# The first norm's modulation by blocks of 128 features, and with each block its rows of the convolution's projections in float32

## The chip, the cores and the metric

The kernel runs on one core of a Trainium2 chip. The metric is the device time of one execution in microseconds (us), the median of three runs. The engines are named as in the profile: PE is TensorE (matmuls; PEld is its weight load), DVE is VectorE, ACT is ScalarE, POOL is GpSimd, and SP is SyncE, which issues the loads.

## The reference

A token matrix x of 256 tokens by 1024 features passes through two layers and then through a second, wider block. Every norm of the two layers is modulated by columns that come from a vector c. Cut to the part that matters here:

```python
c_act = jax.nn.silu(c)
for layer in range(2):
    mod = (c_act @ ada_w[layer] + ada_b[layer])[:, None, :]
    shift_m, scale_m, gate_m, shift_f, scale_f, gate_f = jnp.split(mod, 6, axis=-1)
    h = _rmsnorm(x, norm_g[layer, 0]) * (1.0 + scale_m) + shift_m
    ...                      # layer 0: gated convolution and retention on h @ w_in; layer 1: S5
    x = x + gate_m * mix
    h = _rmsnorm(x, norm_g[layer, 1]) * (1.0 + scale_f) + shift_f
    x = x + gate_f * (jnp.square(jax.nn.relu(h @ w_fc1[layer])) @ w_fc2[layer])
```

`ada_w` has 1024 x 6144 numbers for each layer, so a layer's modulation is 24 MB of float32 weights for six vectors of 1024. In layer 0 `h @ w_in` has 3072 columns; the first 1024 are the convolution's values (512) and its gates (512), the rest are q, k, v and the gate of the retention. The convolution has 31 taps over 512 channels.

## The kernel before

All activations lie with features on the 128 partitions, in eight blocks of 128 features, 256 tokens along the row. A weight is loaded in pieces of 1 MB (`load`, into one of four buffers of the pool `wr`) by SyncE, and split into two float32r parts (`split`, `hilo`): ScalarE rounds a quarter to `hi` (L314), VectorE subtracts to get `lo` (L315), in two buffers each. A projection (`lin`, `mm3`, L319 to L321) is then three matmuls for every block of features and 128 columns, so 48 matmuls for a piece.

A vector of the modulation (`ada`, L434 to L447) is four loads of 1 MB, here called four steps. Each step is eight matmuls into 32 partitions of a PSUM bank (L439); behind the fourth VectorE transposes the sums (L444) and adds the bias (L445). The ten vectors that are not needed at once are a fill (`Fill`): `step_piece` in the mixer makes 1.25 steps of it with every weight piece, the layer norm makes five at its start (`fills[0]`), the feed-forward of layer 0 makes 0.375 with every piece, and a call of `need` makes all steps up to a vector that is about to be used. The vector (1,5) is made in another way, by VectorE, far later.

The program begins with S5's parameters (`s5_prep`, small operations on VectorE and ScalarE, until about 51 us), then the scale and the shift of layer 0 (eight steps), the first norm (`rms`, `normed`), and then `mixer0`: four pieces for the convolution, in PSUM banks of the tag `mm`, with a tanh and a product (L518, L519) behind each pair; the 31 taps of the convolution, two channel blocks on ScalarE and GpSimd (L536, L537) and two on VectorE (L531, L533); eight pieces for q, k, v and the gate; the layer norm over the convolution's channels (L611 are its sums, float32 matmuls of full size); and the output projection. The text numbers the twelve pieces 0 to 11; 4 is the first of q.

What order the engines follow is set by a list scheduler: the code's order is the priority, and an instruction whose inputs are late in the scheduler's own reckoning lets later ones pass. On the chip each engine then takes its list strictly in order, SyncE too.

## Time and profile before

| | us |
|---|---|
| median of the runs | 1231.36 |
| lowest and highest run | 1228.97, 1233.6 |
| span of the profiled execution, from its first to its last instruction | 1227.2 |
| TensorE busy in that span | 1169.7 |
| VectorE busy | 891.7 |
| ScalarE busy | 609.7 |

The profile gives the span of one execution; no time of that very execution is given beside the span. The median of the runs lies 4.2 us above it. A matmul's busy time in the profile overlaps with that of the next one, so TensorE's busy share says whether it had work, and its pace is read from the distance between starts.

### The profile page before, as it was taken

How to read it: one execution, taken by the hardware profiler on the slowest of the kernel's cores; microseconds unless marked ns; L12 is line 12 of the kernel's file. 1: busy time of each engine (PE TensorE's matmuls, PEld its weight loads, DVE VectorE, ACT ScalarE, POOL GpSimd, SP SyncE). 2: the span in 40 equal slices, each digit the busy share in tenths (PEclk: the TensorE clock that was granted, in tenths of full speed). 3: DMA queues.
4: the chain of work that ended last, by engine and by line, in shares of the span. 5: the costliest groups of instructions: out<-in, count | busy, mean ns of one | idle time of the engine just before them, and what ended most of it. 6: DMA issues, size and time to landing. Idle time of an engine off the chain costs nothing. (4 is left out here: it accounts for less than half of the span.)

```text
span 1227.2 us, 25417 instructions
## 1 busy us (share of the span) xinstructions
PE 1169.7 (95%) x10482; PEld 1109.3 (90%) x10482; DVE 891.7 (73%) x1821; ACT 609.7 (50%) x1202; POOL 106.1 (9%) x138
## 2 busy tenths in 40 slices
PE   6899897999999976899999999999999999999998
PEld 4698686999999964899999999999999999999998
DVE  7879888889888859767765656686667686665564
ACT  3577244655555542545544545573465545544441
POOL 0077321000000006200000000000000000000000
PEclk8899997999999977799999999999999999999999
DMA  9888886688888999554466655453443454555541
GB/s 341 340 311 327 297 294 212 238 265 282 297 287 267 300 249 309 216 172 171 169 243 212 233 174 172 164 172 104 151 159 138 172 168 148 194 179 177 194 155 60
DMA packets 69979, 267.29 MB, mean 218 GB/s; under 512 B 7380, under 2 KB 35428, under 8 KB 43240
## 3 DMA queue, kind: packets, MB, share of 16 engines
q1 hardware_dynamic: 69864, 265.68, 63.5%
q8 instruction: 82, 1.34, 0.4%
q14 instruction: 33, 0.27, 0.1%
HBM read 246.85 MB, written 18.81 MB: 216 GB/s over the span
## 5 line engine op out<-in xcount | busy, mean ns | idle before, releaser
L315 DVE TENSOR_TENSOR lo<-w,hi 128x512 fp32r<-128x512 f32 (+1 forms) x640 | 427.6, 712 | 147.7 <-ACT hi L314 147.1
L314 ACT ACTIVATE hi<-w 128x512 fp32r<-128x512 f32 (+1 forms) x640 | 358.4, 625 | 337.0 <-PE mm L320 118.8
L319 PE MATMUL mm<-h,hi 128*128 128x256 f32 x1328 | 379.7, 286 | 0.3 <-ACT h L398 0.3
L320 PE MATMUL mm<-h,hi 128*128 128x256 f32 x1328 | 377.7, 285 | 1.3 <-DVE h L399 1.1
L321 PE MATMUL mm<-h,lo 128*128 128x256 f32 x1328 | 378.6, 285 | 0.0
L319 PEld LDWEIGHTS mm<-h,hi 128*128 128x128 f32 x1328 | 254.7, 192 | 7.2 <-issue 3.4
L320 PEld LDWEIGHTS mm<-h,hi 128*128 128x128 f32 x1328 | 254.6, 192 | 2.8 <-DVE h L399 1.5
L321 PEld LDWEIGHTS mm<-h,lo 128*128 128x128 f32 x1328 | 254.5, 192 | 2.6 <-issue 1.6
L321 PE MATMUL at<-s,lo 128*128 128x256 f32 x720 | 204.4, 284 | 1.7 <-DVE lo L315 1.7
L319 PE MATMUL at<-s,hi 128*128 128x256 f32 x720 | 204.8, 284 | 0.0
L320 PE MATMUL at<-s,hi 128*128 128x256 f32 x720 | 204.1, 284 | 0.0
L321 PEld LDWEIGHTS at<-s,lo 128*128 128x128 f32 x720 | 137.9, 192 | 2.5 <-DVE lo L315 2.1
L319 PEld LDWEIGHTS at<-s,hi 128*128 128x128 f32 x720 | 138.0, 192 | 1.8 <-issue 1.4
L320 PEld LDWEIGHTS at<-s,hi 128*128 128x128 f32 x720 | 138.0, 192 | 0.6 <-issue 0.6
L439 PE MATMUL fa<-wa,crep 128*32 128x256 f32 x704 | 56.4, 428 | 7.0 <-DMA wa<-in_ada_dram 3.8
L537 POOL TENSOR_TENSOR s<-s,cv 128x256 f32<-128x256 f32 x60 | 49.9, 866 | 38.9 <-ACT cv L536 38.7
L439 PEld LDWEIGHTS fa<-wa,crep 128*32 128x32 f32 x704 | 23.0, 120 | 27.0 <-issue 6.4
L319 PE MATMUL fp<-h,hi 128*128 128x256 f32 x144 | 41.9, 291 | 0.7 <-ACT h L314 0.7
L320 PE MATMUL fp<-h,hi 128*128 128x256 f32 x144 | 41.8, 290 | 0.0
L321 PE MATMUL fp<-h,lo 128*128 128x256 f32 x144 | 41.6, 289 | 0.0
L929 ACT COPY Wt<-fp 128x512 f32<-128x512 f32 x32 | 18.6, 581 | 43.3 <-PE fp L928 39.9
L536 ACT ACTIVATE cv<-ap,s 128x256 f32<-128x256 f32 x60 | 29.5, 506 | 17.2 <-POOL s L537 16.4
(438 smaller groups left out, 1829.6 us busy)
## 6 DMA issues: line engine op xcount, KB each, us to landing
w<-in_fc_dram SPq DMA_DIRECT2D x64, 1024.0 KB, 5.1
wa<-in_ada_dram SPq DMA_DIRECT2D x44, 1024.0 KB, 6.5
w<-in_w_in_dram SPq DMA_DIRECT2D x38, 1024.0 KB, 4.9
w<-in_w_gate_dram SPq DMA_DIRECT2D x11, 1024.0 KB, 5.0
w<-in_w_up_dram SPq DMA_DIRECT2D x11, 1024.0 KB, 4.9
Vd<-V SPq DMA_DIRECT2D x16, 512.0 KB, 6.6
w<-in_w_out_dram SPq DMA_DIRECT2D x8, 1024.0 KB, 6.2
Wd<-Wt SPq DMA_DIRECT2D x16, 512.0 KB, 5.2
```

What stands on the lines that cost most here:

```text
L314: self.nc.scalar.activation(hi, h, AF.Copy)
L315: self.nc.vector.tensor_tensor(lo, h, hi.bitcast(F32), op=ALU.subtract)
L319: mm(ps, sh, mh, start=start, stop=False, skip_group_check=True)
L320: mm(ps, sh, ml, start=False, stop=False, skip_group_check=True)
L321: mm(ps, sl, mh, start=False, stop=stop, skip_group_check=True)
L439: nc.tensor.matmul(ps[32 * q:32 * q + 32], self.crep[:, 2 * k + k2], w[:, n:n + 256], start=k == 0 and k2 == 0, stop=k == 3 and k2 == 1, t ...
L536: nc.scalar.mul(t, src, w)
L537: nc.gpsimd.tensor_tensor(acc[:, ch], acc[:, ch], t, op=ALU.add)
L929: nc.scalar.copy(W[:, :, k], pt.rearrange("p (e x) -> p e x", e=4))
```

## The change

The two steps "modulation" and "norm and the convolution's projections" are woven into one loop over the eight feature blocks (`first`). For a block c it loads the block's columns of scale and shift (`ada_c`, 1 MB) and the block's 128 rows of the convolution's 1024 weight columns (`w_in_a`, 0.5 MB, in a whole buffer of `wr`). It makes 256 modulation sums (eight matmuls, L494), copies them out on ScalarE (L496), turns them into two columns by two one-column matmuls against a vector that picks one row in 32 (L498), adds bias and gain on VectorE (L499, L500), norms the block (L502, L503), and adds the block's product with its weight rows into four PSUM banks, eight float32 matmuls (L505), without a split of the weights. The rounded h for the retention is made from the same h. The sums over all eight blocks are the convolution's values and gates (`pa`), and `mixer0` begins with the tanh on them. The first step of S5's preparation now comes ahead of all this in the code and the rest behind it. Lines move by 4 up to `ada`, and by more further on.

```diff
+    a = f(v["ada_w"])[0].reshape(8, 128, 6, 8, 128)[:, :, 0:2]
+    d["ada_c"] = con(a.transpose(3, 1, 0, 2, 4).reshape(8, 128, 2048))
+    d["w_in_a"] = con(f(v["w_in"])[0][:, 0:1024].reshape(8, 128, 1024))
...
+    def first(self, x, r):
+        nc = self.nc
+        pick = self.keep([128, 1], "pick")
+        nc.gpsimd.memset(pick, 0.0)
+        for q in range(4):
+            nc.gpsimd.memset(pick[32 * q:32 * q + 1], 1.0)
+        g = self.keep([128, 8], self.name("modg"))
+        cols = self.ps("mm")
+        pa = [self.pair("at") for _ in range(4)]
+        h32 = self.wh.tile([128, 2048], F32R, name="h32", tag="hi").bitcast(F32).rearrange("p (c t) -> p c t", c=8)
+        hh, hl = self.sb([128, 8, T], F32R, "h"), self.sb([128, 8, T], F32R, "h")
+        ab = self.col("ada_b", 0, 16)
+        for c in range(8):
+            wa = self.load(self.I["ada_c"][c].rearrange("p (k n) -> p k n", k=8), 8, 256)
+            w = self.load(self.I["w_in_a"][c].rearrange("p (k n) -> p k n", k=1), 1, 1024)
+            ps = self.ps(("fa", "fp")[c % 2])[:, 0:256]
+            for k in range(8):
+                q = 32 * (k % 4)
+                nc.tensor.matmul(ps[q:q + 32], self.crep[:, k], wa[:, k], start=k < 4, stop=k >= 4, tile_position=(0, q))
+            t = self.sb([128, 256])
+            nc.scalar.copy(t, ps)
+            for i in range(2):
+                nc.tensor.matmul(cols[:, 2 * c + i:2 * c + i + 1], t[:, 128 * i:128 * i + 128], pick, start=True, stop=True)
+            nc.vector.tensor_tensor(self.mod[0][:, c:c + 9:8], cols[:, 2 * c:2 * c + 2], ab[:, c:c + 9:8], op=ALU.add)
+            nc.vector.scalar_tensor_tensor(g[:, c:c + 1], self.mod[0][:, 8 + c:9 + c], 1.0, self.col("norm_g", c), op0=ALU.add, op1=ALU.mult)
+            h = self.sb([128, T])
+            nc.vector.scalar_tensor_tensor(h, x[:, c], g[:, c:c + 1], r, op0=ALU.mult, op1=ALU.mult)
+            nc.scalar.activation(h32[:, c], h, AF.Identity, bias=self.mod[0][:, c:c + 1])
+            for b in range(8):
+                nc.tensor.matmul(pa[b // 2][:, b % 2], w[:, 0, 128 * b:128 * b + 128], h32[:, c], start=c == 0 and b % 2 == 0,
+                                 stop=c == 7 and b % 2 == 1, skip_group_check=True)
+            self.hilo(hh[:, c], hl[:, c], h32[:, c])
+        return (hh, hl), pa
...
-    def mixer0(self, x, h, fill, need, after_conv, each):
+    def mixer0(self, x, h, pa, fill, need, after_conv, each):
...
         for j in range(2):
-            pv, pg = self.pair(), self.pair()
-            self.lin(pv, step_piece("w_in", j), h, K8)
-            self.lin(pg, step_piece("w_in", 2 + j), h, K8)
+            pv, pg = pa[j], pa[2 + j]
             t = self.sb([128, 2, T])
             nc.scalar.activation(t, pg, AF.Tanh, scale=0.5)
...
+            prep.step()
+            self.mark("first")
+            self.pc_tag = self.pb_tag = "mm"
+            h, pa = self.first(x, self.rms(x))
+            self.pc_tag = self.pb_tag = "at"
             self.mark("prep")
             prep.drain()
...
-            Fill(self.ada(0, 1), self.ada(0, 0)).drain()
...
-                h = self.normed(x, self.rms(x), self.modg(0, 1, 0), self.modv(0, 0))
...
-                self.mixer0(x, h, ada, lambda: need(0, 2), begin, lambda j: st.add(x))
+                self.mixer0(x, h, pa, ada, lambda: need(0, 2), begin, lambda j: st.add(x))
```

The four pieces that leave `mixer0` took five steps of the fill with them, so the fill's later calls find more left. What the scheduler makes of it on the engines is read from the built programs. Names carry a number for each tile; xN is a row repeated N times.

**TensorE at the start.** Before, behind the norm's sums (L167) come four steps of the scale, the spread of the norm's factor (L369), four of the shift and the first step of the fill:

```order
L439 MATMUL fa_367<-wa_368,crep 32x256 x8
L167 MATMUL at_468<-inv_99,q_479 128x1 x4
L439 MATMUL fa_367<-wa_378,crep 32x256 x8
L439 MATMUL fa_367<-wa_388,crep 32x256 x8
L439 MATMUL fa_367<-wa_398,crep 32x256 x8
L369 MATMUL at_503<-ident,s_491 128x128 x2
L439 MATMUL fa_411<-wa_412,crep 32x256 x8
L439 MATMUL fa_411<-wa_422,crep 32x256 x8
L439 MATMUL fa_411<-wa_432,crep 32x256 x8
L439 MATMUL fa_411<-wa_442,crep 32x256 x8
```

Now (behind the same sums, of which the first three groups and two modulations stand ahead of these rows) `fa` and `fp` hold a block's modulation sums, `mm_213` the columns, `at_214` to `at_217` the four banks; `w_285` and `w_317` are the modulation weights of blocks 2 and 3, `w_223` and `w_255` the weight rows of blocks 0 and 1:

```order
L494 MATMUL fa_289<-w_285,crep 32x256 x8
L373 MATMUL mm_203<-ident,s_191 128x128 x2
L498 MATMUL mm_213<-pick,s_234 128x1 x2
L498 MATMUL mm_213<-pick,s_266 128x1 x2
L494 MATMUL fp_321<-w_317,crep 32x256 x8
L505 MATMUL at_214<-h_218,w_223 128x256 x2
L505 MATMUL at_215<-h_218,w_223 128x256 x2
L505 MATMUL at_216<-h_218,w_223 128x256 x2
L505 MATMUL at_217<-h_218,w_223 128x256 x2
L498 MATMUL mm_213<-pick,s_298 128x1 x2
L505 MATMUL at_214<-h_218,w_255 128x256 x2
L505 MATMUL at_215<-h_218,w_255 128x256 x2
```

The matmuls of block 0 (`w_223`) stand behind the modulation sums of block 3 (`w_317`), and from there blocks take turns with one another's modulation.

**SyncE at the start.** The loads behind the first four and three small ones of S5; `ada_c` and `w_in_a` alternate, and they share the four buffers of `wr`, each waiting for the buffer that comes free first:

```order
L302 DMA w_285<-in_ada_c_dram 128x2048
L302 DMA w_287<-in_w_in_a_dram 128x1024
L302 DMA w_317<-in_ada_c_dram 128x2048
L302 DMA w_319<-in_w_in_a_dram 128x1024
L302 DMA w_349<-in_ada_c_dram 128x2048
L302 DMA w_351<-in_w_in_a_dram 128x1024
L302 DMA w_381<-in_ada_c_dram 128x2048
L302 DMA w_383<-in_w_in_a_dram 128x1024
L302 DMA w_413<-in_ada_c_dram 128x2048
L302 DMA w_415<-in_w_in_a_dram 128x1024
L302 DMA w_445<-in_ada_c_dram 128x2048
L302 DMA w_447<-in_w_in_a_dram 128x1024
```

Before, nine loads of `in_ada` and the first of `in_w_in` stood in the place of these; the loads of the fill and of piece 4 (`w_983`) now come behind block 7's.

**TensorE at the end of S5.** `fp` is the last gated projection, L167 (L171 now) the sums of the next norm, `mhh` and `mhl` the memory, whose projection fills the time of that norm. Before:

```order
L321 MATMUL fp_6750<-h_6223,lo_6766 128x256
L167 MATMUL at_6611<-inv_99,q_6743 128x1 x4
L319 MATMUL mm_6948<-mhh,hi_6951 128x256
L320 MATMUL mm_6948<-mhl,hi_6951 128x256
L321 MATMUL mm_6948<-mhh,lo_6952 128x256
```

Now:

```order
L171 MATMUL at_6470<-inv_99,q_6602 128x1 x4
L443 MATMUL fa_6741<-wa_6742,crep 32x256 x8
L443 MATMUL fa_6741<-wa_6752,crep 32x256 x8
L443 MATMUL fa_6741<-wa_6762,crep 32x256 x8
L443 MATMUL fa_6741<-wa_6772,crep 32x256 x8
L171 MATMUL at_6470<-inv_99,q_6735 128x1 x4
L323 MATMUL mm_6851<-mhh,hi_6854 128x256
L324 MATMUL mm_6851<-mhl,hi_6854 128x256
```

The four steps of the vector (1,4) have come between them, and the last group of the norm's sums ahead of the memory's projection.

**SyncE at the same place.** Before, the loads of three memory pieces follow the last gated piece:

```order
L298 DMA w_6763<-in_glu_b_dram 128x2048
L298 DMA w_6949<-in_w_mkv_dram 128x2048
L298 DMA w_7043<-in_w_mkv_dram 128x2048
L298 DMA w_7137<-in_w_mkv_dram 128x2048
L298 DMA w_7223<-in_fc_1_dram 128x2048
```

Now the four of `in_ada` stand ahead of them:

```order
L302 DMA w_6622<-in_glu_b_dram 128x2048
L439 DMA wa_6742<-in_ada_dram 128x2048
L439 DMA wa_6752<-in_ada_dram 128x2048
L439 DMA wa_6762<-in_ada_dram 128x2048
L439 DMA wa_6772<-in_ada_dram 128x2048
L302 DMA w_6852<-in_w_mkv_dram 128x2048
L302 DMA w_6946<-in_w_mkv_dram 128x2048
```

The first memory piece can go into a buffer only when one of these four is used up.

## Rows read from the trace of the kernel before

**Rows 1.** The page: its first line, and TensorE busy and GB/s by slices.

```profile
span 1227.2 us, 25417 instructions
PE   6899897999999976899999999999999999999998
GB/s 341 340 311 327 297 294 212 238 265 282 297 287 267 300 249 309 216 172 171 169 243 212 233 174 172 164 172 104 151 159 138 172 168 148 194 179 177 194 155 60
```

**Rows 2.** TensorE by stretches: length, busy (rows), granted clock, DMA share, GB/s.

```profile
14.00:42.00 28.00, 19.38 (x172) 0.75 1.00 384
42.00:70.00 28.00, 28.00 (x240) 0.95 0.88 321
```

**Rows 3.** Timeline of TensorE: start, duration, line, names, rows merged, idle before.

```profile
14.07 1.93 PE L439 MATMUL fa<-wa,crep 128*32 128x256 f32 x16
35.44 1.93 PE L439 MATMUL fa<-wa,crep 128*32 128x256 f32 x16 [3.11 <-DVE s L444]
39.99 1.93 PE L439 MATMUL fa<-wa,crep 128*32 128x256 f32 x14 [2.62 <-DMA wa<-in_ada_dram]
41.85 0.58 PE L319 MATMUL mm<-h,hi 128*128 128x256 f32 x1
```

**Rows 4.** The same timeline at pieces 0 to 4.

```profile
55.62 1.93 PE L439 MATMUL fa<-wa,crep 128*32 128x256 f32 x32
63.43 1.07 PE L439 MATMUL fa<-wa,crep 128*32 128x256 f32 x16
70.37 1.93 PE L439 MATMUL fa<-wa,crep 128*32 128x256 f32 x32
72.23 0.39 PE L319 MATMUL mm<-h,hi 128*128 128x256 f32 x1
```

**Rows 5.** Line 611: ns min/median/max, first and last start.

```profile
L611 PE MATMUL at<-s,inv x8: 379/379/382, 150.2 to 151.7; 128*128 128x256 f32 x8
```

**Rows 6.** TensorE in slices of 2 us, columns as in the second group.

```profile
22.00:24.00 2.00, 0.13 (x4) 1.00 1.06 410
24.00:26.00 2.00, 0.98 (x4) 0.61 0.93 315
44.00:46.00 2.00, 2.00 (x15) 0.77 0.59 152
```

**Rows 7.** Timeline of SyncE's queue: the second batch of modulation loads.

```profile
16.06 12.43 SPq L435 DMA_DIRECT2D wa<-in_ada_dram  x5
```

**Rows 8.** The page, DMA issues: count, size, median us to landing.

```profile
w<-in_fc_dram SPq DMA_DIRECT2D x64, 1024.0 KB, 5.1
```

**Rows 9.** Timelines of ScalarE and VectorE, early stretch and layer norm.

```profile
28.55 0.61 ACT L813 ACTIVATE tiny<-Wt 64x512 f32<-64x512 f32 x1
...
35.80 2.04 DVE L397 SCALAR_TENSOR_TENSOR s<-x,modg,at 128x256 f32<-128x256 f32 x5
...
159.52 0.16 DVE L347 TENSOR_TENSOR s<-s,s 128x2 f32<-128x2 f32 x1
```

**Rows 10.** Busy table of VectorE during the convolution.

```profile
78.00:142.00 64.00, 61.96 (x118) 1.00 0.77 281
```

**Rows 11.** GpSimd's groups from 50 to 125 us: busy, mean ns, idle.

```profile
L537 POOL TENSOR_TENSOR s<-s,cv 128x256 f32<-128x256 f32 x60 | 49.9, 866 | 38.9 <-ACT cv L536 38.7
```

**Rows 12.** Timeline of VectorE: the convolution's last operations.

```profile
141.01 0.83 DVE L533 SCALAR_TENSOR_TENSOR s<-ap,s,fp 128x256 f32<-128x256 f32 x2
```

**Rows 13.** Timelines of SyncE, TensorE and ScalarE where S5 ends.

```profile
530.85 12.73 SPq L298 DMA_DIRECT2D w<-in_w_mkv_dram  x3
550.81 18.46 SPq L298 DMA_DIRECT2D w<-in_fc_dram  x4
...
558.10 0.95 PE L167 MATMUL at<-inv,q 128*128 128x1 f32 x8
558.91 0.36 PE L319 MATMUL mm<-mhh,hi 128*128 128x256 f32 x1
...
562.72 0.63 ACT L155 ACTIVATE q<-x 128x512 f32<-128x512 f32 x1 [1.87 <-DVE x L1141]
```

More of the change, by code (lines that the diff above doesn't have):

```diff
@@ L1567, in build @@
             prep = Fill(self.s5_prep())
-            if self.lam_first:
-                prep.step()
             nc.sync.dma_start(x, self.I["x"])
+            prep.step()
[3 more added lines that the diff above has]
+            self.pc_tag = self.pb_tag = "at"
             self.mark("prep")
@@ L1586, in begin @@
                         self.tc.add_manual_dep(i, ends[i.engine], info)
-            self.mark("ada0")
-            Fill(self.ada(0, 1), self.ada(0, 0)).drain()
             order = [(0, k) for k in (2, 3, 4, 5)] + [(1, k) for k in range(6)]
@@ L1594, in build @@
             with self.phase(s4=self.m4, ap=1, cv=self.ncv):
-                self.mark("norm0")
-                h = self.normed(x, self.rms(x), self.modg(0, 1, 0), self.modv(0, 0))
                 self.mark("mixer0")
                 st = Sums(self)
-                self.mixer0(x, h, ada, lambda: need(0, 2), begin, lambda j: st.add(x))
+                self.mixer0(x, h, pa, ada, lambda: need(0, 2), begin, lambda j: st.add(x))
                 need(0, 4)
```

## The prediction

> **What bounds the kernel now.** I read the page from the top first. Its span and the busy slices of PE [rows 1] show a kernel that TensorE fills, except in the first slices and in a few short dips. The busy table of stretches says the same with numbers: 19.4 of 28 us between 14 and 42 us, at a mean granted clock of 0.75, then all 28 us between 42 and 70 [rows 2]. So before 42 us TensorE has about a third of its time free, and from there on a microsecond of its work is about a microsecond of span. The loads are the other limit of that first stretch, at 384 GB/s [rows 2].
>
> Then the timeline of TensorE at the start [rows 3]: the matmuls of `ada` (L439) come piece by piece, the last with 2.62 us of waiting for its load, and the first matmul of a projection begins at 41.85 us. The timeline goes on [rows 4]: the four weight pieces of the convolution's projections with fills of `ada` between them, until the first matmul of piece 4 (q of the retention; I call its end "q0") at 72.23 us. Its 48 matmuls at 0.12 us end at 78.0 us. This is the mark for all that follows: what does the change do to q0's end, and what is left undone by then? Up to it seven steps of later `ada` work have run, 16 rows each: one at 35.44, one at 39.99 (14 rows, two more behind), two at 55.62, one at 63.43, two at 70.37 [rows 3, 4].
>
> **Prices.** A step of `ada` (8 matmuls) takes 1.93 us at the low level (35.44) and 0.97 at the full one (two in 1.93 us at 55.62) [rows 3, 4]. A float32 matmul of full size with 256 columns, such as the change puts in, has two rows in the trace. Those of L611 start from 150.2 to 151.7, seven gaps of 0.214 us, so 0.43 us a matmul [rows 5], at the full clock; at half the clock 0.86. Four one-column matmuls took 0.95 us [rows 13], so a pair 0.48.
>
> **Removed and added at the start.** Gone after 42 us are 192 matmuls at 0.12 us, 23.0 us. Added are 64 x 0.43 = 27.5 us of float32 matmuls, 8 x 0.48 for the columns, and per block a copy and a rounding on ScalarE and two tiny operations on VectorE, where 16 splits on each of these engines go. The loads are the same bytes. TensorE thus does more, but earlier: the question is when the last block is through.
>
> I walk the order of TensorE. The copy of block 1's modulation stands on ScalarE behind the three activations L849 to L851 (L811 to L813 before), which end at 28.55 + 0.61 = 29.2 us [rows 9]. They wait for VectorE's preparation of S5, which the change does not shorten. The copy takes 0.5, block 1's columns 0.9 at the low clock: 30.6. Then block 3's modulation, 1.93: block 0's float32 matmuls begin at 32.5 us. By then the loads of blocks 0 to 2 are there (block 2's modulation is issued where the second batch of `ada` was, at 16.06 [rows 7]).
>
> Work from there: 27.5, four modulations 3.9, six pairs 2.9, together 34.3 us. The clock is low at that moment, since a slice with 0.13 of 2 us busy at 22 us was followed by its fall, and it came back some 3 us after the work of 41.85 us began [rows 6]: 3 us at half pace lose 1.5. Waits: from a block's columns to its float32 matmuls lie three VectorE operations (two steps of 0.2 as between 159.52 and its neighbours, one of 0.41) and one on ScalarE, about 1.5 us with the hand-overs [rows 9]. One modulation (0.97) stands between, which leaves 0.5 for blocks 4 to 6, 1.5 in all. A load's landing is 5.1 us [rows 8]. A modulation's load waits for the float32 matmuls three blocks back, and TensorE has 4.9 to 5.9 us of other work in that time, so I charge nothing. For block 7 I charge 2.2: its activation stands on ScalarE behind the first rounding of piece 4, whose load is issued only after block 7's modulation and shares the queue with another megabyte. Blocks done: 32.5 + 34.3 + 1.5 + 3.7 = 72.0; the 46 matmuls left of q0 at 0.12 are 5.5; q0's end 77.5 against 78.0. **Term 1: -0.5 us.** Bounds: without the waits and the low clock -5.7, at the low clock throughout (34.3 once more, less the 1.5 counted) about +32.
>
> **What is put off.** By q0's end one step of `ada` has run now, not seven. Before, the mixer made 12 x 1.25 + 5 = 20 steps up to the layer norm; now its eight pieces make 10 + 5. The order shows where the rest goes. One lands beyond the layer norm's sums or in the mixer more than before (1.0), one in the first feed-forward (1.0), and four stand together behind the last gated projection of S5. **Terms 2 and 3: +2.0 us.** The convolution is why I give nothing back for the quieter mixer. Its first channels could start on GpSimd when two pieces were through; now all start together behind block 7, at 72.0 + 0.6 + 0.7. GpSimd's 60 additions (49.9 us, and some 14 of waits while they run) [rows 11] then end near 138 us, under the 141.8 us at which VectorE ends its share [rows 12]. VectorE is busy 61.96 of the 64 us before that [rows 10]. It starts 2 us later and has one split (four operations, 2.5 us) less in front: no change, with a margin of 4 us to GpSimd.
>
> **At the end of S5.** Now the loads of three memory pieces are issued from 530.85 and those of the feed-forward from 550.81. TensorE goes from the last gated projection at once into the memory's projections at 558.91 [rows 13]. In the changed order the four loads of `ada` (1,4) take the first places, the last being issued about 550.81 and landed 5.1 later [rows 8], in time. TensorE spends 4 x 0.97 = 3.9 until 562.8. The last sums wait for ScalarE's square of 562.72 + 0.63 and end at 564.2. But the memory's first piece can be loaded only into a buffer that the first step gives back, at 559.9: landed 565.0, rounded 565.7. The memory begins 6.8 us later than 558.91 with 0.85 us of sums already done. **Term 4: +5.9 us.** Bounds 3.9 (all waits hidden) and 8 (one landing more).
>
> **Sum:** -0.5 + 2.0 + 5.9 = +7.4 us, span 1234.6 for 1227.2 [rows 1]. The runs' median 1231.4 is 4.2 above that span; with it **1239 us**.
>
> **The rivals.**
> *The loads set the pace (faster).* If the blocks came as fast as the queue moved 384 GB/s [rows 2], 12 MB behind x (landed near 8 us) would be in by 40 us, the last block through at 45, q0 at 50, 28 us sooner; VectorE would begin the convolution 25 us sooner, and with 7.9 given back that is 17 us less: 1214. For it speaks the third of TensorE that is free before 42. Against it: the order puts block 0's matmuls behind block 3's modulation, and from block 3 on the loads wait for buffers. 0.17.
> *Neither end matters (same).* Term 1 at its low bound, -5.7, and term 4 at 3.9: with terms 2 and 3 about +0.2, 1232. 0.25.
> *The clock stays low (slower by far).* Every float32 block waits for one to two hand-overs, and if TensorE then ran at 1.2 GHz, a block's matmuls would take 6.9 us, not 3.4: up to 32 more, 1270. Against it: in the trace the clock fell after a slice that was nearly empty and held where the work was dense [rows 6], and here some nine tenths of a block are work. It decides from about half the blocks on, at 1254. The Trainium skill (TensorE: Matmul & The Clock Gate, Loop structure matters more than you think) warns of this shape, a loop that waits for a load before each bundle of matmuls and so lets the array go cold; by that rule the low clock would be the case, while the fall at 24 us agrees only for long waits. 0.1.
> *The forecast*, 0.48, with its own range 1233 to 1247.
>
> **Numbers.** One in ten left out at each side: the low end cuts the loads' case at 1218, the high end cuts the clock's at 1254. A difference under 0.5% (6 us) can hardly be told from none here. The forecast lies just past that line, so about 0.3 of its 0.48 counts as slower and the rest as the same; with the clock's case, and a little of the neutral one on each side: faster 0.18, same 0.37, slower 0.45.
>
> **What would show it.** Block 0's float32 matmuls at about 32.5 us and rows of 0.21 us apart from 36 us on; the last block's near 72 and q0's end near 78; GpSimd's additions from about 74 to 138; the layer norm's sums (L611 before) within 2 us of 150; four steps of `ada` at about 560 us and a gap of 1 to 2 us behind them. I am wrong if block 0 starts before 28 us, if the clock column stays near 0.5 between 36 and 72, if the layer norm waits for GpSimd, or if the memory's first piece is already there when the four steps end.

## The result and the profile after

| | before | changed |
|---|---|---|
| median of the runs, us | 1232.28 | 1252.47 |
| lowest and highest run, us | 1228.97, 1233.60 | 1247.21, 1255.13 |
| ratio, 95% interval | | 1.0163, 1.0133 to 1.0192 |
| span of the profiled execution, us | 1227.2 | 1251.9 |

The kernel became slower by 20.2 us, where 7.4 were forecast. The profiled spans differ by 24.7. The changed kernel's profiled execution took 1253.66 us, 1.8 more than its span; with as much beside its span, that of before was as fast as its fastest run.

The page of the changed kernel, answering to [rows 1]:

```profile
span 1251.9 us, 25367 instructions
PE   5999898999999966799999999999999999999998
GB/s 242 219 296 322 303 253 278 195 276 279 310 262 283 294 237 308 207 202 238 169 207 265 203 195 168 178 163 98 159 145 155 148 169 169 169 191 180 181 165 60
```

The dip in the fifteenth to seventeenth slice is a little deeper than before (6 6 7 for 7 6 8), and the first two GB/s figures are 242 and 219, for 341 and 340: a queue that waits. TensorE by the stretches of [rows 2], same columns:

```profile
14.00:42.00 28.00, 22.27 (x127) 1.00 0.52 175
42.00:70.00 28.00, 24.68 (x176) 1.00 0.80 273
```

Up to 42 us the loads move 175 GB/s, not 384. The timeline of TensorE (start, duration, line, names, rows merged, idle before), answering to [rows 3, 4]:

```profile
31.95 5.62 PE L505 MATMUL at<-h,w 128*128 128x256 f32 x16
37.77 3.70 PE L505 MATMUL at<-h,w 128*128 128x256 f32 x16
...
62.77 1.07 PE L494 MATMUL fp<-w,crep 128*32 128x256 f32 x16 [1.14 <-DMA w<-in_ada_c_dram]
...
68.69 1.07 PE L443 MATMUL fa<-wa,crep 128*32 128x256 f32 x16 [0.86 <-DMA wa<-in_ada_dram]
71.74 0.39 PE L323 MATMUL mm<-h,hi 128*128 128x256 f32 x1 [1.98 <-ACT hi L318]
...
72.14 3.72 PE L505 MATMUL at<-h,w 128*128 128x256 f32 x16
...
81.09 0.28 PE L325 MATMUL mm<-h,lo 128*128 128x256 f32 x1
```

Block 0's float32 matmuls begin at 31.95 and take 5.5 us, the next block 3.6; the last block's begin at 72.14, behind a wait for a load (62.77), a step of `ada` (68.69, with its own wait) and 1.98 us for the first rounding of piece 4 (71.74, in front of two matmuls of q0). q0 ends at 81.2, not 78.0.

At the layer norm, TensorE's and then VectorE's timeline, answering to [rows 5, 12]:

```profile
154.90 1.74 PE L373 MATMUL at<-ident,s 128*128 128x128 f32 x8 [3.25 <-DVE s L353]
156.43 3.02 PE L649 MATMUL at<-s,inv 128*128 128x256 f32 x8
...
147.33 0.87 DVE L571 SCALAR_TENSOR_TENSOR s<-ap,s,fp 128x256 f32<-128x256 f32 x2
149.36 1.18 DVE L348 TENSOR_SCALAR s<-s 128x4 int32<-128x4 int32 x1
```

The convolution's last tap ends at 148.2 (before 141.8) and the sums start at 156.43 (before 150.15), behind the retention's second spread, which waits 3.25 us for VectorE's chain L348 to L353.

S5 goes through eight parts, called pairs, each with tables that SyncE loads (`Wt`, `Mt` and `Vt` in the rows). First three rows of the kernel before (TensorE at norm 1's last sums, its longest wait for a table or a load, SyncE's queue at the table of pair 1), then the same places of the changed one, where a left-over load of `ada` stands on the queue ahead of the table:

```profile
436.64 1.16 PE L167 MATMUL at<-inv,q 128*128 128x1 f32 x8 [0.92 <-ACT q L155]
490.86 0.65 PE L1079 MATMUL at<-Mt,s 128*32 128x128 f32 x8 [3.21 <-DMA Mt<-Kd]
...
415.29 1.65 SPq L1001 DMA_DIRECT2D Wt<-Wd  x2
```

```profile
423.29 0.33 SPq L439 DMA_DIRECT2D wa<-in_ada_dram  x1
428.89 0.80 SPq L1039 DMA_DIRECT2D Wt<-Wd  x2
...
445.25 1.05 PE L171 MATMUL at<-inv,q 128*128 128x1 f32 x8
475.40 1.29 PE L1075 MATMUL mm<-Wt,s 128*32 128x128 f32 x16 [10.67 <-DMA Wt<-Wd]
```

From norm 1's last sums to the end of the gated projections it took 121.5 us (558.10 less 436.64 [rows 13]); now it takes 128.0 (573.27 below less 445.25), with a wait of 10.67 us for a table where the longest for a table or load was 3.2.

Where S5 ends, TensorE's timeline, answering to [rows 13]:

```profile
573.27 0.95 PE L171 MATMUL at<-inv,q 128*128 128x1 f32 x8
574.15 3.66 PE L443 MATMUL fa<-wa,crep 128*32 128x256 f32 x64
577.74 1.05 PE L171 MATMUL at<-inv,q 128*128 128x1 f32 x8
580.88 0.39 PE L323 MATMUL mm<-mhh,hi 128*128 128x256 f32 x1 [2.09 <-ACT hi L318]
...
582.77 0.41 PE L325 MATMUL mm<-mhh,lo 128*128 128x256 f32 x1
```

Four steps of `ada` (64 rows), then 2.09 us for the memory's first rounding; and from 581.94 to 585.33 us the rows stand 0.21 us apart, about half the pace. The granted clock reads 0.50 from 582 to 585 us, the lower level. SyncE's queue shows what the rounding waited for: the memory's first load is issued at 575.28, when the first of the four steps has given its buffer back.

```profile
575.28 2.06 SPq L302 DMA_DIRECT2D w<-in_w_mkv_dram  x3
```

Summed over the trace, the changed kernel is later by 3.2 us at q0's end, 8.6 at norm 1's last sums, 15.2 at the end of the gated projections, 22.0 at the memory's first matmul and 24.7 at the end.

### The profile page after: what moved, and what is told of

Read it like the earlier page. It is cut to its first block, busy times and chain, and to the rows that moved or that the text cites. A ratio compares the mean times of both kernels' runs of the same rounds, so it can differ in the third digit from the quotient of the medians.

```text
span 1251.9 us, 25367 instructions
## 1 busy us (share of the span) xinstructions
PE 1182.3 (94%) x10450; PEld 1119.3 (89%) x10450; DVE 884.0 (71%) x1816; ACT 608.1 (49%) x1202; POOL 106.5 (9%) x143
## 5 line engine op out<-in xcount | busy, mean ns | idle before, releaser
L318 ACT ACTIVATE hi<-w 128x512 fp32r<-128x512 f32 (+1 forms) x624 | 349.6, 625 | 334.5 <-PE mm L324 113.1
L319 DVE TENSOR_TENSOR lo<-w,hi 128x512 fp32r<-128x512 f32 (+1 forms) x624 | 411.1, 702 | 140.7 <-ACT hi L318 140.2
L323 PE MATMUL mm<-h,hi 128*128 128x256 f32 x1264 | 361.8, 286 | 3.4 <-ACT hi L318 2.3
L325 PE MATMUL mm<-h,lo 128*128 128x256 f32 x1264 | 361.6, 286 | 1.1 <-DVE lo L319 1.1
L324 PE MATMUL mm<-h,hi 128*128 128x256 f32 x1264 | 360.2, 285 | 2.3 <-DVE h L403 2.1
L323 PEld LDWEIGHTS mm<-h,hi 128*128 128x128 f32 x1264 | 242.9, 192 | 9.0 <-ACT hi L318 4.1
L324 PEld LDWEIGHTS mm<-h,hi 128*128 128x128 f32 x1264 | 243.1, 192 | 3.7 <-DVE h L403 2.3
L325 PEld LDWEIGHTS mm<-h,lo 128*128 128x128 f32 x1264 | 243.2, 192 | 2.9 <-DVE lo L319 1.5
L443 PE MATMUL fa<-wa,crep 128*32 128x256 f32 x576 | 42.6, 391 | 1.6 <-DMA wa<-in_ada_dram 1.6
L318 ACT ACTIVATE s<-s 128x512 fp32r<-128x512 f32 (+1 forms) x49 | 30.0, 612 | 11.7 <-DVE s L699 4.4
```

Source lines behind the costliest of these rows:

```text
L318: self.nc.scalar.activation(hi, h, AF.Copy)
L319: self.nc.vector.tensor_tensor(lo, h, hi.bitcast(F32), op=ALU.subtract)
L323: mm(ps, sh, mh, start=start, stop=False, skip_group_check=True)
L324: mm(ps, sh, ml, start=False, stop=False, skip_group_check=True)
L325: mm(ps, sl, mh, start=False, stop=stop, skip_group_check=True)
L443: nc.tensor.matmul(ps[32 * q:32 * q + 32], self.crep[:, 2 * k + k2], w[:, n:n + 256], start=k == 0 and k2 == 0, stop=k == 3 and k2 == 1, t ...
```

## The experiments

Marks of every profiled execution, from TensorE's timelines: the start of the layer norm's sums, of norm 1's last sums, from these to the sums behind the last gated projection (S5), and from there to the memory's first matmul (gap). "Put off" says what stands where: L, the load of one step of `ada` that is left over when the first feed-forward ends, ahead of S5's tables; E, four steps at S5's end. The marks come from one execution of each kernel, the medians from four to six; the ratio is to executions of the kernel before that were taken with it, with medians from 1230.4 to 1232.3. The edits are shown shortened, with `...` for what is left out.

| kernel | put off | median us | ratio to before, 95% | layer norm | norm 1 | S5 | gap |
|---|---|---|---|---|---|---|---|
| before | - | 1232.28 | | 150.15 | 436.64 | 121.5 | 0.81 |
| changed | L, E | 1252.47 | 1.0163 (1.0133 to 1.0192) | 156.43 | 445.25 | 128.0 | 7.61 |
| a_one | E | 1253.97 | 1.0181 (1.0150 to 1.0212) | 153.96 | 442.93 | 131.6 | 7.63 |
| a_five | - | 1266.23 | 1.0273 (1.0253 to 1.0293) | 166.55 | 460.06 | 135.4 | 0.81 |
| a_ln10 | - | 1255.25 | 1.0188 (1.0159 to 1.0216) | 155.43 | 460.17 | 124.9 | 0.82 |
| b_less5 | L, E | 1245.86 | 1.0103 (1.0081 to 1.0126) | 155.12 | 442.23 | 126.5 | 7.56 |
| a_pin | L, E | 1250.09 | 1.0155 (1.0125 to 1.0184) | 154.85 | 445.10 | 125.8 | 7.48 |
| a_buf_pin | L, E | 1254.36 | 1.0186 (1.0162 to 1.0209) | 157.04 | 450.35 | 125.0 | 7.69 |
| a_buf_fill_pin | - | 1254.26 | 1.0179 (1.0155 to 1.0203) | 168.68 | 456.87 | 125.8 | 0.81 |
| a_split_pin | L, E | 1249.26 | 1.0153 (1.0132 to 1.0174) | 156.42 | 443.00 | 129.8 | 7.60 |
| a_one_act | E | 1250.92 | 1.0151 (1.0127 to 1.0175) | 155.77 | 445.36 | 123.0 | 7.56 |
| b_left1 | L | 1239.79 | 1.0067 (1.0043 to 1.0092) | 151.72 | 442.47 | 127.1 | 0.81 |
| a_taps | L, E | 1251.92 | 1.0168 (1.0143 to 1.0194) | 158.08 | 447.20 | 126.2 | 7.50 |
| a_split_one | E | 1243.00 | 1.0091 (1.0067 to 1.0115) | 155.25 | 441.71 | 121.7 | 7.76 |

The theory at the outset: most of the 20 us comes from the steps of `ada` that the change puts off, because the mixer has four weight pieces fewer that bring steps with them. The rival: the block loop delays everything, and what is seen in S5 only follows. Single executions of one kernel lie up to 14.6 us apart (a_one), so I read nothing into a difference of two such medians under some 4 us.

**a_one.** One step more in the layer norm.

```diff
-        self.fills = (5, 0, 0, 0)
+        self.fills = (6, 0, 0, 0)
```

> The changed kernel with one step of the later modulation more in the layer norm (six in place of five), so that feed-forward 0 ends without a left-over step. The four steps of vector (1,4) stay behind the last gated projection of S5. Theory 'put-off steps': the left-over step's load stood ahead of S5's table loads and changed their order on SyncE's queue; without it the table of pair 2 is loaded ahead of that of pair 3 again, the wait of 10.7 us in S5 goes, S5 (from norm 1's sums to the end of its gated projections) takes about 130 us, not 137, and the whole about 1245 us. Rival 'the block loop delays all': S5's loads are late because everything before is; the wait stays, and the time is within 2 us of the changed kernel's 1252.

The time did not move, and S5 became longer. The table of pair 1 is now issued at 421.70, 3.6 us behind the table's store at 418.14 (3.2 in the kernel before), and no wait for a table exceeds 2.34 us. But ScalarE's list came out in another order. ScalarE's and TensorE's timelines:

```profile
504.57 2.19 ACT L318 ACTIVATE hi<-w 128x512 fp32r<-128x512 f32 x4 [12.81 <-DMA w<-in_glu_a_dram]
506.67 0.56 ACT L1077 COPY s<-mm 128x512 f32<-128x512 f32 x1
...
507.28 1.11 PE L1081 MATMUL at<-ident,s 128*128 128x128 f32 x4 [11.40 <-ACT s L1077]
```

The rounding of the first gated weight stands ahead of the last chunk states' copy (L1077), waits 12.81 us for its load, and the copy, TensorE and the scan wait with it. So this run says nothing for or against the theory's price.

**a_five.** The five steps back into the mixer, ahead of S5.

```diff
-        self.rates = (1.25, ...)
+        self.rates = (1.875, ...)
...
         need()
+        self.rate = 1.25
```

> The changed kernel with five steps of the later modulation more in the mixer (1.875 with each of the eight weight pieces there, not 1.25), so that all vectors but one are made before S5, as in the kernel before. Theory 'put-off steps': both S5's order of table loads and its end are as before; of the 24.7 us by which the profiled spans differ, 7.3 in S5 and 7.8 at its end go, and the five steps cost at most 4.8 us where the mixer is full: between 1237 and 1243 us. Rival 'the block loop delays all': only the 7.8 us at S5's end can go, less 4.8: about 1249.

Both theories fail here, by 17 us and more. At the end of S5 all is as the theory had it, TensorE's timeline:

```profile
595.42 0.95 PE L171 MATMUL at<-inv,q 128*128 128x1 f32 x8
596.23 0.36 PE L323 MATMUL mm<-mhh,hi 128*128 128x256 f32 x1
```

But norm 1's last sums come at 460.06, 14.8 us later than in the changed kernel, for five steps of 0.97 us, and ScalarE's accident in S5 comes again (16.20 us for a load). The last weight piece of the gate is issued at 137.68 us there, at 123.47 in the changed kernel. The busy table from 80 to 120 us, a_five and then the changed kernel (PE, PEld, DVE, ACT, POOL busy, clock, DMA share, GB/s):

```profile
80.00:120.00 40.00, 36.19 (x345) 28.63 (x344) 37.91 (x65) 26.72 (x54) 31.62 (x38) 1.00 0.87 334
```

```profile
80.00:120.00 40.00, 38.63 (x350) 33.56 (x349) 39.43 (x62) 27.68 (x57) 31.97 (x35) 1.00 0.81 307
```

The queue moves more (334 against 307 GB/s) and TensorE does less (36.2 against 38.6 us). Each step brings a load of 1 MB, 2.7 us at the 384 GB/s of [rows 2]; five are 13.6 us, close to the 14.8. That these loads are the cause fits the rows, and was not tried apart: only 10.1 of the 14.8 us are lost up to the layer norm's sums, and behind them, from 200 to 240 us, the granted clock is 0.74, for 0.83 in the changed kernel.

**a_ln10.** The five steps at the start of the layer norm.

```diff
-        self.fills = (5, 0, 0, 0)
+        self.fills = (10, 0, 0, 0)
```

> The changed kernel with the same five steps, all at the start of the layer norm (ten there, not five), where TensorE waits for VectorE's end of the convolution. Theory 'put-off steps': as with the steps in the mixer, and the steps lie beside VectorE's work if their loads are there in time: 1235 to 1240 us. Rival: the loads of five more steps come one after the other there, about 3 us each, and the layer norm's sums start later by some 5 us: about 1245.

Slower than either figure, and not where the rival had it: the sums start no later (155.43), but norm 1's come 14.9 us later than in the changed kernel, as in a_five. At either place in the mixer the five steps cost some 15 us, and what they win in S5 (3.1 here) and at its end (6.8) does not pay for that.

**b_less5.** The kernel before, with five steps fewer.

```diff
-        self.rates = (1.25, ...)
+        self.rates = (0.834, ...)
...
         need()
+        self.rate = 1.25
```

> The kernel before with five steps of the later modulation fewer in the mixer (0.834 with each of its twelve weight pieces, not 1.25), nothing of the block loop. S5's table loads then stand on SyncE's queue as in the changed kernel (pair 3's ahead of pair 2's), and four steps come behind S5's last gated projection. Theory 'put-off steps': plus 14 us for S5 and its end, less up to 4.8 that the mixer saves: 1241 to 1246 us. Rival 'the block loop delays all': S5 waits for no table here; plus 6 at S5's end less 4.8: about 1233.

The theory's range holds it: 14.3 us without a line of the block loop. TensorE's timeline shows both places, the table in S5 and the memory at its end:

```profile
472.67 1.08 PE L1038 MATMUL mm<-Wt,s 128*32 128x128 f32 x16 [10.46 <-DMA Wt<-Wd]
...
576.31 0.51 PE L319 MATMUL mm<-mhh,hi 128*128 128x256 f32 x1 [2.04 <-ACT hi L314]
```

So putting the steps off costs, in the kernel before, more than two thirds of what the change costs. But it does not cost it only where the theory says. In the profiled execution S5 is 5.0 us longer and its end 6.8, and norm 1's last sums come 5.6 us later (5.0 of it up to the layer norm), where the theory had up to 4.8 us less, since the mixer has five steps fewer. That its range holds is in part luck, and why a mixer with fewer steps takes longer is not taken apart.

**a_pin.** S5's order tied down in the changed kernel.

```diff
...
+            with self.held_at(wlast):
                 Wt = wide("Wt", self.wplace[ip], ip)
+            wlast[SP] = self.last(SP)
...
+                states = self.last(Activation)
...
-            scanned = {DVE: self.last(DVE)}
+            scanned = {DVE: self.last(DVE), Activation: states}
```

> The changed kernel with S5's order tied down: each pair's first table is issued on SyncE's queue behind that of the pair before it, and the first rounding of the gated projections' weights stands on ScalarE behind the last of the chunk states' copies. Nothing else is changed; the five steps stay put off. Theory 'order of S5': from norm 1's last sums to the end of the gated projections it takes about 121.5 us again, as in the kernel before, not 128, and the whole about 1246 us. Rival 'the queue of S5 is full': the tables come no sooner in another order, and another wait of some 7 us stands in the place of the 10.7 us one: 1250 to 1253 us.

The rival holds. The pairs are issued in their order, and waits stay: 7.46 us for a table, and 4.40 for another, which the trace puts down to the load beside it:

```profile
471.98 1.08 PE L1077 MATMUL mm<-Wt,s 128*32 128x128 f32 x16 [7.46 <-DMA Wt<-Wd]
...
504.70 0.66 PE L1119 MATMUL at<-Mt,s 128*32 128x128 f32 x8 [4.40 <-DMA m<-in_mem_dram]
```

The order of pairs 2 and 3, which I had blamed, makes at most 2.2 of the 6.5 us (S5 takes 125.8, for 128.0). What a_pin keeps is the left-over load ahead of pair 1: the table is issued at 428.73, 5.6 us behind that load, 9.4 behind the store.

**a_buf_pin.** The same, with five buffers of their own for the blocks' weight rows.

```diff
-            w = self.load(self.I["w_in_a"][c]...)
+            w = own.tile([128, 1024], F32, ...)      # a pool of five
+            nc.sync.dma_start(w, self.I["w_in_a"][c]...)
```

> S5's order tied down as in a_pin, and the eight loads of the convolution's weight rows get five buffers of their own, 4 KB a partition, so that a load of the block loop no longer waits for the float32 matmuls of two or three blocks before. Theory 'SyncE's queue stands idle while the blocks run': between 28 and 42 us it moves over 300 GB/s, not 114, the waits of some 5 us between the blocks go, and q0 ends near 77 us, not 81: about 4 us under a_pin. Rival 'TensorE's own work paces the blocks': loads come early and q0's end moves by less than 1 us, so does the whole.

The queue does fill, and no time is won. Busy table, and TensorE's timeline:

```profile
14.00:28.00 14.00, 8.17 (x64) 4.57 (x56) 13.39 (x71) 5.15 (x14) 0.00 (x0) 0.86 1.03 414
28.00:42.00 14.00, 13.17 (x70) 9.51 (x70) 12.66 (x44) 5.99 (x17) 0.24 (x2) 0.77 0.65 238
```

```profile
60.01 0.61 PE L501 MATMUL mm<-pick,s 128*128 128x1 f32 x4 [1.60 <-ACT s L499]
...
72.92 3.62 PE L508 MATMUL at<-h,wi 128*128 128x256 f32 x16
```

414 and 238 GB/s, where the changed kernel has 237 and 114; no block waits for a load; and yet the last block begins at 72.92, for 72.14 in the changed kernel and 71.40 in a_pin. Each block takes TensorE 3.6 us, its modulation 1.0 and its columns 0.5, and one block waits 1.60 us for ScalarE (60.01) and then runs at half the pace (5.2 us, granted clock 0.50 from 62 to 65 us). So far the rival holds: early loads alone win nothing. The wait and the slow block together are worth some 3 us, so that the run does not show what early loads would win without them. The whole is 4.3 us slower than a_pin, with intervals that overlap.

**a_buf_fill_pin.** The same, with the five steps inside the block loop.

```diff
-            ps = self.ps(("fa", "fp")[c % 2])[:, 0:256]
+            ps = self.ps("fp" if c >= 2 else ("fa", "fp")[c % 2])[:, 0:256]
...
             self.hilo(hh[:, c], hl[:, c], h32[:, c])
+            if c in (2, 3, 4, 5, 6):
+                fill.step()
```

> As a_buf_pin, and the five steps of the later modulation that were put off are made in the block loop, one behind each of the blocks 2 to 6, where the queue has room. Theory 'a put-off step costs its load, 2.7 us, once the mixer's queue is full, and only its matmuls, 1 us, where the queue idles': q0 ends some 5 us later than in a_buf_pin, the end of S5 gets its 6.8 us back and 1 us of low clock more: 2 to 4 us under a_buf_pin. Rival 'a step costs its load everywhere': q0 13 us later than in a_buf_pin, the whole 5 us slower than that.

The steps need one of the two PSUM banks, so from block 2 on the modulation sums have the other alone. In the block loop a step costs what the theory says (the last block begins at 77.16, 4.2 us later, for five), and S5's end gets its 6.9 us back. The sum is still no better, because the layer norm's sums start 11.6 us later than in a_buf_pin. Part of it is VectorE's order: the product that the convolution starts from is done at 81.3, and the first running sum of a tap on VectorE (L577) stands behind eight weight splits and the first rotation of q, at 94.47, where in the changed kernel it came at 82.50.

**a_split_pin.** Float32r parts in the block loop, S5 tied down.

```diff
...
-            for b in range(8):
-                nc.tensor.matmul(pa[b // 2][:, b % 2], w[...], h32[:, c], ...)
+            wh, wl = self.split(w, 1, 1024)
+            for b in range(8):
+                self.mm3(pa[b // 2][:, b % 2], wh[...], wl[...], hh[:, c], hl[:, c], ...)
```

> S5's order tied down as in a_pin, and the blocks' products made with float32r parts, three matmuls of 0.12 us for one float32 matmul of 0.44: each block's weight rows are rounded on ScalarE and subtracted on VectorE, which have little to do between 42 and 70 us, and a weight buffer comes free with that. Theory 'the blocks are paced by TensorE and by the buffers': a block takes 2.9 us, not 3.6, the waits for loads shrink, and q0 ends 5 us or more before a_pin's 81: about 1240 us. Rival 'the chain through ScalarE and VectorE paces them': the split's 2.4 us on either engine come between a block's norm and its matmuls, and q0 ends no sooner.

The blocks are through 5.5 us sooner, as the theory has it (the last row at 69.2, for 74.7 in a_pin), q0 ends 4.2 us sooner and the first product of k and q comes 5.2 us sooner. But the layer norm does not come sooner: at 142.71 TensorE waits 4.37 us for VectorE, whose tiny steps of the retention's norm take 0.86 to 1.16 us there, beside GpSimd (see a_taps). S5 waits 12.18 us for a table, and the time is that of a_pin within the intervals, not the theory's 1240.

**a_one_act.** a_one with ScalarE's order tied down, as in a_pin.

> The changed kernel with one step more in the layer norm, as a_one, so that no left-over load stands ahead of S5's tables, and with the first rounding of the gated projections' weights behind the last chunk states' copy on ScalarE, so that a_one's wait of 11.4 us can't come. Theory 'one left-over load ahead of the tables': S5, from norm 1's last sums to the end of the gated projections, takes 121 to 123 us as in the kernel before (121.5), not 128; the whole 1245 to 1247 us. Rival 'S5's queue is full whatever stands in it': S5 takes 126 us or more, as in a_pin.

S5 takes 123.0 us in the profiled execution, as the theory says, and that execution's span is 5.0 us under the changed kernel's. The median is only 1.5 under it, above the expected range; the intervals overlap. By itself this run does not decide.

**b_left1.** The kernel before with a single step fewer.

```diff
-        self.fills = (5, 0, 0, 0)
+        self.fills = (4, 0, 0, 0)
```

> The kernel before with one step of the later modulation fewer at the start of the layer norm (four, not five). One step is then left over when feed-forward 0 ends; its load stands on SyncE's queue right ahead of the table of pair 1, and pair 3's table ahead of pair 2's, as in the changed kernel. Nothing of the block loop, and no step behind the gated projections. Theory 'one left-over load ahead of the tables': S5 takes 126 to 129 us, not 121.5, and the whole 1236 to 1239 us. Rival 'a single load of 1 MB': at most its own 2.7 us, 1230 to 1234 us.

One step fewer costs 8.3 us (5.3 to 11.3), more than the theory's 5 to 8 and far more than its load. SyncE's queue and TensorE:

```profile
416.69 0.43 SPq L932 DMA_DIRECT2D Wd<-Wt  x1
420.48 0.33 SPq L435 DMA_DIRECT2D wa<-in_ada_dram  x1
426.10 0.80 SPq L1001 DMA_DIRECT2D Wt<-Wd  x2
...
474.17 1.08 PE L1037 MATMUL mm<-Wt,s 128*32 128x128 f32 x16 [11.66 <-DMA Wt<-Wd]
```

The left-over load comes 3.8 us behind the store of the table, of which it waits 3.3 for a buffer; the table behind it comes 5.6 later still, and pair 2's table is missing for 11.66 us. S5 is 5.6 us longer, which is what this run shows of the load. 5.8 us had been lost up to norm 1, 5.1 of it before that load was issued (a step of `ada` in the first feed-forward begins at 404.8, for 399.7). Behind the layer norm's sums the clock differs: the busy table from 150 to 220 us, of the kernel before and then of this one (columns as above):

```profile
150.00:220.00 70.00, 61.72 (x565) 54.90 (x565) 58.74 (x116) 34.95 (x77) 15.02 (x10) 0.90 0.71 251
```

```profile
150.00:220.00 70.00, 60.44 (x512) 53.38 (x511) 50.68 (x108) 27.85 (x62) 14.60 (x10) 0.80 0.64 231
```

The granted clock is 0.80, for 0.90, an estimated 7 us of work at the full level, enough for the loss. So one load ahead of the tables is worth 5.6 us here, and not the whole 8.3. Why one step fewer in the layer norm lets it fall for longer I can't derive.

**a_taps.** 16 tap operations fewer on VectorE.

```diff
+                    if own and 10 <= tau < 18:
+                        continue
```

> The changed kernel without 8 of the 31 taps of the convolution on the two channel blocks that VectorE sums (its result there is another): 16 operations of 0.45 us fewer on VectorE, nothing else. Theory 'VectorE is full from the last block's end to the layer norm': the convolution ends 7 us sooner, near 140.5 us, the layer norm's sums start near 150, and the whole comes 5 to 7 us under the changed kernel, 1246. Rival 'the loads or TensorE pace the mixer': VectorE is done sooner and waits, the sums start at most 2 us sooner, 1251 us.

The theory's forecast fails. VectorE's taps end 10 us sooner, at 137.8, and the layer norm's sums start at 158.08, 1.7 us later than in the changed kernel. GpSimd's, VectorE's and TensorE's timelines:

```profile
142.02 1.21 POOL L921 TENSOR_TENSOR tv<-bc,tiny 128x576 f32<-128x576 f32 x1
...
142.11 1.14 DVE L350 SCALAR_TENSOR_TENSOR s<-s,s 128x4 f32<-128x4 f32 x1
155.79 0.16 DVE L353 SCALAR_TENSOR_TENSOR s<-s,s 128x4 f32<-128x4 f32 x1
...
146.25 1.13 PE L619 MATMUL at<-s,s 128*128 128x256 f32 x4 [3.36 <-DVE s L617]
...
158.08 1.89 PE L651 MATMUL at<-s,inv 128*128 128x256 f32 x8
```

With the taps gone, VectorE comes to the retention's norm while GpSimd is at its last additions and then at S5's outer products, and of nine tiny steps four take 0.65 to 0.68 us, one 0.39 and four 1.14, where 0.16 is usual. That is some 6 us, about what the taps had freed, so the run does not show what VectorE's taps would be worth without this collision. It shows that the sums stand on TensorE behind that norm (L619, then L1232 and its spread), not behind the convolution alone.

**a_split_one.** Float32r parts, one step more, ScalarE's order: the parts that were worth something.

> What the runs so far favour, together: float32r parts in the block loop (q0 ended some 5 us sooner with them), one step more in the layer norm, and ScalarE's order in S5 tied down. The four steps at S5's end stay. If the left-over load made S5 long and VectorE's start sets the layer norm, S5 takes 122 us and the layer norm's sums start near 154: about 1243 us, still slower than the kernel before. If S5 is as long as before without the left-over load, 1249.

The time came as expected. Against a_split_pin, which has the left-over load and SyncE's order tied down besides, S5 is 8.1 us shorter and the time 6.3 (the intervals are apart). Against a_one_act, which differs only in its float32 blocks, the time is 7.9 shorter, also with intervals apart; but in the two profiled executions the layer norm's sums come only 0.5 us sooner (155.25, not the 154 expected). Another 3.1 us are won from there to norm 1, where the granted clock from 150 to 220 us is 0.93, for 0.83. No version beats the kernel before: the four steps at S5's end and some 5 us of the mixer remain.

## Why the prediction was right, and where it was wrong

The direction and the range held, but the time lies just under the range's upper end, above the forecast's own 1233 to 1247, and the change cost 20.2 us where the sum has 7.4. That it lies inside is luck: the upper end, 1254, was set by the rival of the low clock, and it is not the clock that made the time long (it reads 1.00 from 42 to 70 us, where that rival has the low level). Right in size was term 4. What failed is the walk of the block loop (term 1), the step "no change" for the layer norm, and S5, for which the sum has nothing.

**Term 1 (-0.5, measured +3.2).** The walk to block 0 was right: 31.95 for 32.5. From there to the end of the last block it took 43.6 us, not 39.5. One step of `ada` between the blocks (68.69) is not in the sum, 1.0; and "I charge nothing" for loads was wrong, since three waits cost 2.6 (0.64 at 56.56, 1.14 at 62.77, 0.86 at 68.69). What I charged for the low clock (1.5, measured 1.9) and for block 7 (2.2, measured 1.98) stood; of the 1.5 for blocks 4 to 6 only 0.30 came (51.87). A block's eight matmuls took 3.55 us, not 3.44, which is 0.9 over eight blocks.

**Terms 2 and 3 (+2.0, measured 5.4 up to norm 1).** The count was right: 240 rows of `ada` lie between q0's end and the layer norm's sums where 224 lay, one step, and the left-over step stands ahead of norm 1's last sums. What was wrong is "no change" for the layer norm, with VectorE starting 2 us later and a margin to GpSimd. VectorE's first running sum of a tap began at 82.50, for 75.1, and its taps ended 6.4 us later; GpSimd's additions ended at 140.7, for the 138 that I had worked out. And the sums do not stand behind the taps, but behind the retention's norm, whose last chain on VectorE begins with L358 (L354 before). Its first row, and a tiny step of the chain ahead of it, before and then changed:

```profile
135.38 0.15 DVE L347 TENSOR_TENSOR s<-s,s 128x4 f32<-128x4 f32 x1
...
144.53 0.16 DVE L354 TENSOR_SCALAR s<-at 128x4 f32<-128x4 f32 x1
```

```profile
137.63 0.38 DVE L351 TENSOR_TENSOR s<-s,s 128x4 f32<-128x4 f32 x1
...
148.69 0.15 DVE L358 TENSOR_SCALAR s<-at 128x4 f32<-128x4 f32 x1
```

The chain begins 4.2 us later: the retention's sums that it reads come 2.2 us later (TensorE, 145.60 for 143.44), and the last taps now stand ahead of it. It takes 1.6 us longer, 1.0 of it in the one step at 149.36. With 0.5 for the spread, part of it at half the pace, this is the 6.3 us by which the sums start later, 3.1 more than q0's end. GpSimd has a part in this that the prediction did not see: before, its additions ended at 122 and its outer products at 133, ahead of this norm; now they end at 140.7 and 150.5, beside it. Behind the sums 2.3 us more are lost up to norm 1: 1.1 because the sums themselves run at half the pace behind the wait of 3.25 us (3.02 us for 1.89, granted clock 0.50 from 155.4 to 158.4 us), and 1.0 for the left-over step. b_less5 comes 5.6 us later at norm 1 without the block loop, so it is not shown how much of the changed kernel's 8.6 us there the loop itself costs.

**S5 (nothing in the sum, measured 6.6).** This is the term that was missing. I counted the left-over step's matmuls, and not that its load stands on SyncE's queue ahead of S5's tables, several of which come through the same four buffers. b_left1 shows it best, since it differs from the kernel before in nothing else: 5.6 us in S5. The pair a_split_one and a_split_pin agrees; a_pin shows that the order of pairs 2 and 3 is at most a third of it. How far one load carries isn't settled: a_ln10 and a_buf_fill_pin have no left-over load, and still take 124.9 and 125.8 us with a wait of 5 to 6 us for a table.

**Term 4 (+5.9, measured 5.9).** The memory began 6.8 us later behind its projections' end than before, with 0.95 us of sums done in between, and it waited for what the prediction names: its first load could be issued only when the first step's buffer came free (575.28). Not in the sum is the slow stretch behind the wait of 2.09 us: 16 matmuls in 3.4 us instead of 1.9.

**The rivals.** The loads did not set the pace, since a_buf_pin, with the loads early, has its last block no sooner. The clock did not stay low: from 37.8 us on the blocks ran at 3.6 us, 2.4 GHz by their pace, through waits of up to 1.98 us, and the granted clock reads 1.00 from 42 to 70 us. But it can fall there: in a_five, a_ln10 and a_taps, whose block loop is the same, the last block took 4.9 to 5.4 us, not 3.7, behind waits of 1.73 to 1.99 us, and the granted clock is 0.83 over the ten us around it. The rule of the Trainium skill (TensorE: Matmul & The Clock Gate, Loop structure matters more than you think) speaks of a "long DMA wait between every matmul"; the waits of this loop, at most 2 us ahead of a bundle of 3.6, are not that case, so it is neither borne out nor refuted here.

## What to carry to other kernels

When a change removes carriers of background work (weight pieces that each bring a step), count where every step goes that they carried, and cost it by what it does to the load queue and the buffers at that place, not by its matmuls. A step whose matmuls take 1 us cost some 0.9 us up to the end of the block loop, some 3 us in the mixer, and 5.6 us of S5 as a single load ahead of a table. And before work is taken off an engine that looks full, ask which instruction the next stage really stands behind, and what that one will run beside: VectorE's taps ended ten microseconds sooner, and its next steps lost the gain beside GpSimd.

## What the runs showed of the hardware

A tiny VectorE operation with two inputs from SBUF (128 x 4) took 0.15 us alone, 0.38 to 0.68 us beside GpSimd's additions of 0.74 to 0.88 us, and 1.14 us beside GpSimd's outer products of 1.21 us: about one product's length each. The Trainium skill (SBUF — State Buffer, SBUF: two separate sides) has the two engines share a pair of ports that one holds for a whole instruction; the row at 142.11 us agrees with it. In the changed kernel even an operation with one input took 1.18 us (149.36) and ended with GpSimd's product beside it.

The granted clock reads 1.00 from 14 to 42 us in the changed kernel, while a step of `ada` takes 1.93 us until 31.95 and 1.07 later, and block 0 takes 5.5 us against 3.6. In a_buf_pin, whose first block begins at 31.6 with a duration of 5.0 us, the column has 0.86 and 0.77 for the same stretches. The trace's own records of the clock begin at 35.8 us in the changed kernel and at 20.7 us in a_buf_pin, and the column reads 1.00 where there is no record. So in the first 42 us the pace of equal instructions has to be read beside the column.
